# Row sums of squares for grouped-query heads: folded to 64 rows, two token tiles per product, issued in two groups

## The chip, the cores and the metric

The kernel runs on one core of a Trainium2 chip. The metric is device time in microseconds of one execution, the median of three. TensorE is called PE, VectorE DVE, ScalarE ACT, GpSimd POOL, SyncE SP, as in the profile.

## What is computed

One step of a two-layer backbone over 640 tokens (512 latent, 128 prompt), width 1024. Layer 0 mixes with latent attention and neighbourhood attention, layer 1 with grouped-query attention; each layer ends in a gated feed-forward block. The change lies in the attention of layer 1. Cut to that, the reference is:

```python
def odd_project(h, w_in, q_norm, k_norm):
    p = h @ w_in
    q, k, v = jnp.split(p, [...], axis=-1)
    q = rms_norm(q.reshape(b, L, GQA_HEADS, GQA_HEAD_DIM), q_norm)
...
def odd_mixer_latent(h, c_k, c_v, ...):
    q = apply_rope(q, cos, sin)
    k = apply_rope(k, cos, sin)
    o = attend_blocked(q, jnp.concatenate([k, c_k], axis=1),
                       jnp.concatenate([v, c_v], axis=1), GQA_SCALE)
```

There are 8 query heads of 128 features and 2 key heads. Each query row is divided by the root of its mean square. The kernel doesn't divide the queries: the factor of each token goes into the softmax, as the scale of the exponential.

## The kernel before

Features lie on the 128 partitions and the 640 tokens along the free axis, in two halves of 320 columns. A product in full precision is three products of split operands: each operand is kept as a high part and a low part in a rounded 32-bit type, and high*high, high*low and low*high add up in one PSUM bank. All products are recorded through one helper (line 64), all transposes through another (line 68), so PE's instructions are told apart by their tiles.

Layer 1's attention runs head by head. In the loop of head h the PE program holds pieces of three heads, in an order written out by hand as a string, `GQA_ORDER`:

```python
GQA_ORDER = "s0 r x0 t0 q0 s1 t1 q1 t2 s2 q2 v0 t3 s3 q3 v1 t4 s4 pt q4 v2 q5 q6 v3 q7 v4 pv"
```

- `s0` to `s4` are the scores of head h for five tiles of 128 tokens (tiles 0 to 3 latent, 4 prompt). Each writes a double bank `gs`; there are two of these, taken in turn, so `s2` waits until the exponential of tile 0 has read its bank. DVE takes the row maximum `gn` (lines 1873, 1879), a DVE product with the factor gives the bias `gb` (line 1883), and ACT writes the exponential `gp` (line 1884). `x0` is this second part of tile 0, kept apart in the string. In `s1` to `s4` it follows the scores directly.
- `q0` to `q7` project the queries of head h+1 (function `gqa_q`): four pieces for token columns 0 to 319, four for 320 to 639. After each half ACT copies the bank to `gqc` (line 1844) and squares the copy into `gsq` (line 1845). DVE applies the rotary tables in four instructions (`gqr`, lines 1748 to 1751, three of them before the closing addition), ACT rounds the result to `gqh` (line 1848), DVE takes the rest `gql` (line 1849).
- `r` sums the squares of head h over the 128 features: for each token tile a product whose stationary operand is the 128x128 block of `gsq` and whose moving operand is two columns of ones. These are plain 32-bit products, two passes each, so five products make ten passes, `gr`. ACT turns the sums into the factor `rq` by a logarithm and an exponential (lines 1856, 1857).
- `t0` to `t4` and `pt` transpose the probabilities of head h-1 (`gt`, `gtp`), ACT and DVE split them (`gts`, lines 401 and 405), and `v0` to `v4` and `pv` multiply them with the values (`go`, `gop`). POOL scales the probabilities beforehand (line 393).

Head 0 has no head before it, so its loop holds no `t` and no `v` piece. Its own queries are projected ahead of the loop. Head 7 has no head after it and holds no `q` piece. The compiler's scheduler orders each engine's own instructions from this program; each engine then works its queue in order.

## Time and profile before

| | us |
|---|---|
| runs | 1473.85, 1476.87, 1478.32 |
| median | 1476.87 |
| the profiled execution's own time | 1476.32 |
| its span, from the first to the last instruction | 1474.5 |
| PE busy | 1440.2 (98% of the span) |
| DVE busy | 1236.9 (84%) |
| ACT busy | 785.2 (53%) |
| grouped-query heads on PE, first scores to the first output projection | 849.5 to 987.4 |

Times in the rows further down are microseconds from the span's start. In a row of the timeline the first number is the start, the second how long the instructions of that row took together, and `[0.26 <-...]` behind it is how long the engine stood idle before it and what released it. PE's instructions overlap: a product of 320 columns is shown with 0.31 us, but the next one starts 0.15 us after it. What a product takes from the path is therefore read from one start to the next.

### The profile page before, as it was taken

To read this page: it belongs to the slowest core of one execution; us is meant where nothing else is said; L and a number is where in the kernel's file an instruction comes from. 1 tells how busy PE (TensorE), PEld (TensorE's weight loads), DVE (VectorE), ACT (ScalarE), POOL (GpSimd) and SP (SyncE) were. 2 spreads that over 40 slices of the span, in tenths; PEclk is the share of its full clock that TensorE was granted. 3 is DMA by queue.
4 is the path that set the end of the run, shared out by engine and by line. 5 is a ranking of instruction groups with operands and counts; after the bars stand their busy time and mean duration, and the time that the engine had idled before them with its cause. 6 is when DMAs were issued, how large, how long until landed. Compare 5 with 4: busy or idle time off the path is not lost.

```text
span 1474.5 us, 25830 instructions
## 1 busy us (share of the span) xinstructions
PE 1440.2 (98%) x9764; PEld 1389.8 (94%) x9764; DVE 1236.9 (84%) x2391; ACT 785.2 (53%) x1539; POOL 174.8 (12%) x270
## 2 busy tenths in 40 slices
PE   5999999999999999999999999999999999999997
PEld 3989978889999999999999999989999999999997
DVE  5877788877998888955997878888899898989976
ACT  5446687763755555531223656672656555555443
POOL 0046635420000000000000122220000000000000
PEclk9999999999999999999999999999999999999999
DMA  9644431025165555568764300115245555548572
GB/s 376 211 157 125 144 115 44 15 91 181 48 219 168 172 172 176 167 233 312 240 216 149 101 30 30 44 42 187 84 169 179 182 176 184 174 147 294 185 270 72
DMA packets 79636, 231.48 MB, mean 157 GB/s; under 512 B 8856, under 2 KB 13240, under 8 KB 79128
## 3 DMA queue, kind: packets, MB, share of 16 engines
q1 hardware_dynamic: 77152, 225.43, 45.5%
q10 hardware_dynamic: 1944, 3.48, 0.7%
q8 instruction: 76, 1.25, 0.3%
q0 software_dynamic: 416, 0.93, 0.2%
q14 instruction: 48, 0.39, 0.1%
HBM read 193.15 MB, written 36.66 MB: 156 GB/s over the span
## 4 chain that ended last, share of the span: by engine, by line
PE 86%; DVE 6%; ACT 4%; issue 2%; DMA 1%; POOL 1%; DVEq 0%; ACTq 0%; POOLq 0%; SPq 0%
PE fg L64 20%; PE fd L64 9%; PE fgo L64 5%; PE fo L64 5%; PE fu L64 4%; PE gq L64 4%; PE fdo L64 2%; PE gs L64 2%; PE go L64 2%; PE nq L64 2%; PE nk L64 1%; PE fuo L64 1%; PE gt L68 1%; PE mod L64 1%; ACT mp L1007 1%
## 5 line engine op out<-in xcount | busy, mean ns | idle before, releaser
L1679 DVE SCALAR_TENSOR_TENSOR junk<-wm,cb 128x1024 bf16<-128x1024 f32 x88 | 107.3, 1220 | 5.5 <-DMA wm<-in_wm 4.3
L64 PE MATMUL gq<-h10h,wgq 128*128 128x320 f32 x256 | 66.4, 319 | 0.0
L267 POOL TENSOR_SCALAR h10h<-h10t,gs,mods 128x320 fp32r<-128x320 f32 x4 | 4.0, 1006 | 430.2 <-DVE h10t L261 427.8
L1419 ACT ACTIVATE wY<-s 128x1024 fp32r<-128x1024 f32 x38 | 40.3, 1060 | 26.7 <-PE fg L64 22.5
L1947 POOL TENSOR_TENSOR xr<-xw,fn1rs 128x320 f32<-128x320 f32 x2 | 1.7, 868 | 412.8 <-ACT fn1rs L235 412.8
L1419 ACT ACTIVATE wZ<-s 128x1024 fp32r<-128x1024 f32 x38 | 40.2, 1057 | 19.1 <-PE fd L64 14.1
L1420 DVE TENSOR_TENSOR wZ<-s,wZ 128x1024 fp32r<-128x1024 f32 x38 | 46.4, 1221 | 2.0
L1420 DVE TENSOR_TENSOR wY<-s,wY 128x1024 fp32r<-128x1024 f32 x38 | 46.4, 1220 | 0.3
L64 PEld LDWEIGHTS gq<-h10h,wgq 128*128 128x128 f32 x256 | 45.4, 191 | 0.6
L1528 DVE TENSOR_TENSOR sg<-up,sg 128x640 f32<-128x640 f32 x38 | 31.3, 823 | 15.7 <-ACT sg L1527 14.7
L1527 ACT ACTIVATE sg<-fg 128x320 f32<-128x320 f32 x38 | 16.7, 439 | 48.3 <-PE fg L64 48.3
L1549 ACT ACTIVATE p<-fd 128x320 f32<-128x320 f32 x38 | 16.6, 438 | 46.0 <-PE fd L64 46.0
L64 PE MATMUL gq<-h10l,wgq 128*128 128x320 f32 x128 | 39.7, 311 | 0.0
L1884 ACT ACTIVATE gp<-gs,gb,rq 128x640 f32<-128x640 f32 (+1 forms) x40 | 31.8, 796 | 13.5 <-DVE gb L1883 12.0
L64 PE MATMUL fg<-h01E,wW 128*128 128x320 f32 x228 | 36.6, 309 | 1.5 <-DVE g L1559 1.5
L64 PE MATMUL fg<-h11N,wZ 128*128 128x320 f32 x228 | 36.7, 309 | 0.0
L64 PE MATMUL fg<-h01q,wX 128*128 128x320 f32 x228 | 36.7, 309 | 0.0
L64 PE MATMUL fu<-h11q,wX 128*128 128x320 f32 x228 | 36.6, 309 | 0.0
L64 PE MATMUL fg<-h01N,wZ 128*128 128x320 f32 x228 | 36.6, 309 | 0.0
L64 PE MATMUL fd<-h01q,wZ 128*128 128x320 f32 x228 | 36.6, 309 | 0.0
L64 PE MATMUL fd<-h11q,wZ 128*128 128x320 f32 x228 | 36.6, 309 | 0.0
L64 PE MATMUL fg<-h11q,wX 128*128 128x320 f32 x228 | 36.5, 309 | 0.0
(3421 smaller groups left out, 5303.3 us busy)
## 6 DMA issues: line engine op xcount, KB each, us to landing
wm<-in_wm SPq DMA_DIRECT2D x48, 512.0 KB, 4.1
mraw<-in_wm SPq DMA_DIRECT2D x8, 1024.0 KB, 13.2
mraw<-in_wm SPq DMA_DIRECT2D x14, 512.0 KB, 3.8
wmv<-in_wm0g SPq DMA_DIRECT2D x8, 512.0 KB, 4.2
wm<-in_wm0g SPq DMA_DIRECT2D x8, 512.0 KB, 4.9
ruo<-in_wFO SPq DMA_DIRECT2D x8, 512.0 KB, 4.3
rgo<-in_wFO SPq DMA_DIRECT2D x8, 512.0 KB, 5.6
x<-in_xT SPq DMA_DIRECT2D x8, 320.0 KB, 4.5
```

The source lines that it names most:

```text
L64: cls.last = nc.tensor.matmul(*a, **k)
L68: cls.last = nc.tensor.transpose(*a, **k)
L267: G.tensor_scalar(h[:, c0:c1], t, self.gsl[:, k, 0:1], self.ml[:, self.sh + k, 0:1], ALU.mult, ALU.add)
L1007: exps[h, j] = S.activation(halves(pt), pss[:, :, :HT], AF.Exp, bias=nm, accum_out=ll[:, j:j + 1])
L1419: S.activation(h, src, AF.Copy)
L1420: V.tensor_tensor(w_, src, f(h), ALU.subtract)
L1527: last = S.activation(sg[:, 0:HT], g[:, :HT], AF.Silu, scale=-1.0)
L1528: V.tensor_tensor(sg, up, sg, ALU.mult)
L1549: S.activation(p5, b5[:, :HT], AF.Copy)
L1679: V.scalar_tensor_tensor(junk, raw, 1.0, cb[:, c, :], ALU.mult, ALU.mult, accum_out=mods[l][:, j0 + i, c:c + 1])
L1884: gexp[h, j] = S.activation(dst, src, AF.Exp, bias=nb, scale=rq[:, j:j + 1], accum_out=ll[:, j:j + 1])
L1947: G.tensor_tensor(x[k][:, c0:c1], root[1][k], nrm.rs[:, c0:c1], ALU.mult)
```

## The change

The sum over 128 features is halved on DVE first. ACT squares the two halves of the feature rows (rows 0 to 63 and 64 to 127) into two tiles that both lie on partitions 0 to 63, by two instructions in place of one. DVE adds the two tiles and writes the result of one token tile to partitions 0 to 63 of a new tile `gfold`, that of the next to partitions 64 to 127. A product over 128 rows then sums two token tiles at once: its moving operand `two` has ones in rows 0 to 63 of its first column and in rows 64 to 127 of its second. Five products become three, of which the last (tile 4) has 64 rows. They are issued in two groups: tiles 0 and 1 by a piece `n` at the end of the loop of the head before, tiles 2 to 4 by `r`, which moves behind `q1`. The logarithm and the exponential for the factor run once for each group. The product of maximum and factor, `gb`, moves from DVE to ACT. In the second half `gql` comes behind the additions.

```diff
--- before.py
+++ after.py
@@ -1829,33 +1829,52 @@
     nc.gpsimd.dma_start(o_gv, gvf[:, :256])
 
     gqs, gexp = {}, {}
+    two = gp.tile([P, 2], F32, name="two")
+    V.memset(two, 0.0)
+    for r in range(2):
+        V.memset(two[64 * r:64 * r + 64, r:r + 1], 1.0)
 
     def gqa_q(h):
         get = lazy(lambda: after(gqs[h - 1][3][0] if h > 1 else None, lambda: unit(wGQ[h], 1024, f"wgq{h}", lo="v" if h == 1 else "v")))
         qh = gp.tile([P, T], F32R, tag="gqh", bufs=2, name=f"gqh{h}")
         ql = gp.tile([P, T], F32R, tag="gql", bufs=2, name=f"gql{h}")
         rq = tiny.tile([P, 5], F32, tag="rq", bufs=2, name=f"rq{h}")
-        sq = tmp(f"gsq{h}")
+        sq = [tmp(f"gsq{h}{r}")[0:64] for r in range(2)]
+        fold = gp.tile([P, 3, P], F32, tag="gfold", bufs=2, name=f"gfold{h}")
+        a, b = [t.rearrange("p (j n) -> p j n", n=P) for t in sq]
         gqs[h] = qh, ql, rq, []
+
+        def folded(i, r, j, n):
+            V.tensor_tensor(fold[64 * r:64 * r + 64, i:i + n, :], a[:, j:j + 2 * n - 1:2, :], b[:, j:j + 2 * n - 1:2, :], ALU.add)
         out = []
         for c, (c0, c1) in enumerate(HALF):
             def done(ps, c=c, c0=c0, c1=c1):
                 qc = tp.tile([P, HT], F32, tag="u", bufs=7, name=f"gqc{h}{c}")
                 gqs[h][3].append(S.activation(qc, ps[:, :HT], AF.Copy))
-                S.activation(sq[:, c0:c1], qc, AF.Square)
+                for r in range(2):
+                    S.activation(sq[r][:, c0:c1], qc[64 * r:64 * r + 64], AF.Square)
                 qr = tp.tile([P, HT], F32, tag="u", bufs=7, name=f"gqr{h}{c}")
                 rope(qr, qc, vcol(V_GQ), c, f"gqr{h}{c}")
                 S.activation(qh[:, c0:c1], qr, AF.Copy)
-                V.tensor_tensor(ql[:, c0:c1], qr, f(qh[:, c0:c1]), ALU.subtract)
+                if c == 0:
+                    V.tensor_tensor(ql[:, c0:c1], qr, f(qh[:, c0:c1]), ALU.subtract)
+                    folded(0, 0, 0, 1)
+                    folded(0, 1, 1, 1)
+                else:
+                    folded(1, 0, 2, 2)
+                    folded(1, 1, 3, 1)
+                    V.tensor_tensor(ql[:, c0:c1], qr, f(qh[:, c0:c1]), ALU.subtract)
             out += pieces_of(f"gq{h}{c}", qbank, get, hh, hl, list(range(KT)), c0, c1, done)
 
-        def rstd():
-            pr = bank(f"gr{h}")
-            for j in range(5):
-                PE.matmul(pr[:, 2 * j:2 * j + 2], sq[:, P * j:P * j + P], ones[:, 0:2], start=True, stop=True)
-            S.activation(rq, pr[:, 0:10].rearrange("p (a b) -> p a b", b=2)[:, :, 0], AF.Ln, bias=eps, scale=1.0 / P)
-            S.activation(rq, rq, AF.Exp, bias=lnsc, scale=-0.5)
-        return out + [rstd]
+        def rstd(at):
+            pr = bank(f"gr{h}{at}")
+            for i in ((0,), (1, 2))[at]:
+                rows = slice(0, P if i < 2 else 64)
+                PE.matmul(pr[:, 2 * (i - at):2 * (i - at) + 2], fold[rows, i, :], two[rows], start=True, stop=True)
+            t = rq[:, (0, 2)[at]:(2, 5)[at]]
+            S.activation(t, pr[:, 0:2 + at], AF.Ln, bias=eps, scale=1.0 / P)
+            S.activation(t, t, AF.Exp, bias=lnsc, scale=-0.5)
+        return out + [lambda: rstd(0), lambda: rstd(1)]
 
     def gqa_scores(h, pts):
         v = h // 4
@@ -1880,7 +1899,7 @@
                 dst, n = pt, P
 
             def weigh():
-                V.tensor_tensor(nb, nm, rq[:, j:j + 1], ALU.mult)
+                S.activation(nb, nm, AF.Copy, scale=rq[:, j:j + 1])
                 gexp[h, j] = S.activation(dst, src, AF.Exp, bias=nb, scale=rq[:, j:j + 1], accum_out=ll[:, j:j + 1])
                 softmax_tail(pt, ll[:, j:j + 1], f"gr{h}_{j}", n)
                 pts.append(pt)
@@ -1914,17 +1933,17 @@
         return {"pt": prompt_t, "pv": prompt, **t}
 
     open_y(s=2)
-    *qp, rstd = gqa_q(0)
-    run(qp)
+    *qp, early, rstd = gqa_q(0)
+    run(qp + [early])
     tail, oG = {}, []
-    GQA_ORDER = "s0 r x0 t0 q0 s1 t1 q1 t2 s2 q2 v0 t3 s3 q3 v1 t4 s4 pt q4 v2 q5 q6 v3 q7 v4 pv"
+    GQA_ORDER = "s0 x0 t0 q0 s1 t1 q1 r t2 s2 q2 v0 t3 s3 q3 v1 t4 s4 pt q4 v2 q5 q6 v3 q7 v4 pv n"
     for h in range(8):
         oG.append(gp.tile([P, T], F32, tag="go", bufs=8, name=f"oG{h}"))
         pts = []
         pieces = gqa_scores(h, pts)
         pieces["r"] = rstd
         if h < 7:
-            *qp, rstd = gqa_q(h + 1)
+            *qp, pieces["n"], rstd = gqa_q(h + 1)
             pieces.update(named("q", qp))
         sequence(GQA_ORDER, {**pieces, **tail})
         tail = gqa_values(h, pts, oG[h])
```

On PE, at the start of head 4's loop (`gs4_0` are its first scores, `gop2` the last values of head 2, `gt3` transposes of head 3, `gq5` queries of head 5), the order was before:

```order
L64 MATMUL gs4_0_10977<-gkh1_9590,gqh4_10730 128x320 x2
L64 MATMUL gs4_0_10977<-gkl1_9592,gqh4_10730 128x320 x2
L64 MATMUL gs4_0_10977<-gkh1_9590,gql4_10731 128x320 x2
L64 MATMUL gr4_10986<-ones_86,gsq4_10733 128x2 x5
L68 MATMUL gt3_0_10999<-ident_81,gp3_0_10737 128x128
```

With the change it is:

```order
L64 MATMUL gop2_11012<-gtp2l_10960,gvh5_9719 128x128
L64 MATMUL gr40_11017<-two_9993,gfold4_10778 128x2
L64 MATMUL gs4_0_11031<-gkh1_9590,gqh4_10773 128x320 x2
L64 MATMUL gs4_0_11031<-gkl1_9592,gqh4_10773 128x320 x2
L64 MATMUL gs4_0_11031<-gkh1_9590,gql4_10774 128x320 x2
L68 MATMUL gt3_0_11045<-ident_81,gp3_0_10782 128x128
```

The five products behind the first scores are gone; one stands ahead of them. The other two stand behind the second query piece, in head 0 directly ahead of the scores of tile 2.

On ACT, in head 0 (`gqc01` is the copy of the second half of its queries, `gp0_0` the exponential of its tile 0), the order was before:

```order
L1844 ACTIVATE gqc01_10067<-gq01_10042 128x320
L1845 ACTIVATE gsq0_10000<-gqc01_10067 128x320
L1856 ACTIVATE rq0_9999<-gr0_10095,eps_88 128x5
L1857 ACTIVATE rq0_9999<-rq0_9999,lnsc_90 128x5
L1848 ACTIVATE gqh0_9997<-gqr01_10070 128x320
L1884 ACTIVATE gp0_0_10087,gl0_10079<-gs0_0_10086,gb0_0_10085,rq0_9999 128x640
```

With the change it is:

```order
L1853 ACTIVATE gqc01_10076<-gq01_10051 128x320
L1875 ACTIVATE rq0_10003<-gr00_10090,eps_88 128x2
L1855 ACTIVATE gsq00_10004<-gqc01_10076 64x320
L1855 ACTIVATE gsq01_10005<-gqc01_10076 64x320
L1876 ACTIVATE rq0_10003<-rq0_10003,lnsc_90 128x2
L1858 ACTIVATE gqh0_10001<-gqr01_10080 128x320
L1875 ACTIVATE rq0_10003<-gr01_10152,eps_88 128x3
L1902 ACTIVATE gb0_0_10103<-gn0_0_10102,rq0_10003 128x1
L1876 ACTIVATE rq0_10003<-rq0_10003,lnsc_90 128x3
L1903 ACTIVATE gp0_0_10105,gl0_10095<-gs0_0_10104,gb0_0_10103,rq0_10003 128x640
```

The first exponential now stands behind the logarithm of the second group (`gr01`), which it doesn't need, and behind its own bias `gb0_0`, which was DVE's.

On DVE, in the same place (`gqr01` is the rotary result of the second half, `gn0_0` the row maximum of tile 0), the order was before:

```order
L1750 SCALAR_TENSOR_TENSOR gqr01b_10071<-gqc01_10067,vec_79,tg_9587 64x320
L1873 TENSOR_REDUCE gn0_0_10084<-gs0_0_10086 128x1
L1751 TENSOR_TENSOR gqr01_10070<-gqr01_10070,gqr01b_10071 128x320
L1883 TENSOR_TENSOR gb0_0_10085<-gn0_0_10084,rq0_9999 128x1
L1873 TENSOR_REDUCE gn0_1_10120<-gs0_1_10122 128x1
L1849 TENSOR_TENSOR gql0_9998<-gqr01_10070,gqh0_9997 128x320
```

With the change it is:

```order
L1750 SCALAR_TENSOR_TENSOR gqr01b_10081<-gqc01_10076,vec_79,tg_9587 64x320
L1848 TENSOR_TENSOR gfold0_10006<-gsq00_10004,gsq01_10005 64x256
L1751 TENSOR_TENSOR gqr01_10080<-gqr01_10080,gqr01b_10081 128x320
L1848 TENSOR_TENSOR gfold0_10006<-gsq00_10004,gsq01_10005 64x128
L1892 TENSOR_REDUCE gn0_0_10102<-gs0_0_10104 128x1
L1866 TENSOR_TENSOR gql0_10002<-gqr01_10080,gqh0_10001 128x320
```

The row maximum of tile 0 moved behind two of the new additions and the closing addition of the rotary step.

## Rows read from the trace of the kernel before

**Rows 1.** Page: busy time, share of the span and instructions of each engine.

```profile
PE 1440.2 (98%) x9764; PEld 1389.8 (94%) x9764; DVE 1236.9 (84%) x2391; ACT 785.2 (53%) x1539; POOL 174.8 (12%) x270
```

**Rows 2.** Page: the chain that ended last, shares by engine.

```profile
PE 86%; DVE 6%; ACT 4%; issue 2%; DMA 1%; POOL 1%; DVEq 0%; ACTq 0%; POOLq 0%; SPq 0%
```

**Rows 3.** Stretches: length, then PE, PEld, DVE, ACT, POOL busy, granted clock, DMA share, GB/s.

```profile
842.00:865.00 23.00, 22.37 (x155) 21.41 (x154) 19.00 (x45) 12.76 (x32) 5.07 (x7) 1.00 0.10 29
865.00:869.00 4.00, 4.00 (x20) 3.99 (x20) 2.62 (x6) 2.44 (x6) 0.00 (x0) 0.57 0.22 88
869.00:973.00 104.00, 104.00 (x713) 99.30 (x711) 85.93 (x189) 68.57 (x158) 24.64 (x30) 1.00 0.11 36
```

**Rows 4.** PE's timeline, heads 3 and 4: the ten passes, and what follows them.

```profile
901.70 1.17 PE L64 MATMUL gr<-ones,gsq 128*128 128x2 f32 x10
902.74 0.64 PE L68 MATMUL gt<-ident,gp 128*128 128x128 f32 x4
...
905.32 0.39 PE L64 MATMUL gq<-h10h,wgq 128*128 128x320 f32 x1
...
919.77 1.17 PE L64 MATMUL gr<-ones,gsq 128*128 128x2 f32 x10
```

**Rows 5.** PE's timeline, heads 0 and 1.

```profile
849.52 0.54 PE L64 MATMUL gs<-gkh,gqh 128*128 128x320 f32 x2
...
854.10 0.31 PE L64 MATMUL gq<-h10h,wgq 128*128 128x320 f32 x1
854.55 0.56 PE L64 MATMUL gs<-gkh,gqh 128*128 128x320 f32 x2
...
861.98 0.31 PE L64 MATMUL gq<-h10h,wgq 128*128 128x320 f32 x1
862.52 0.56 PE L64 MATMUL gs<-gkh,gqh 128*128 128x320 f32 x2 [0.23 <-ACT gqh L1848]
...
863.63 0.56 PE L64 MATMUL gs<-gkh,gql 128*128 128x320 f32 x2 [0.26 <-DVE gql L1849]
...
865.05 0.90 PE L68 MATMUL gt<-ident,gp 128*128 128x128 f32 x4
...
869.20 0.39 PE L64 MATMUL gq<-h10h,wgq 128*128 128x320 f32 x1
```

**Rows 6.** DVE's timeline, head 0: row maximum, closing addition of the rotary step.

```profile
851.90 0.82 DVE L1873 TENSOR_REDUCE gn<-gs 128x1 f32<-128x640 f32 x1
852.64 0.48 DVE L1751 TENSOR_TENSOR gqr<-gqr,gqr01b 128x320 f32<-128x320 f32 x1
```

**Rows 7.** ACT's timeline, head 0: the factor's exponential, the first of the softmax.

```profile
852.00 0.30 ACT L1857 ACTIVATE rq<-rq,lnsc 128x5 f32<-128x5 f32 x1
...
853.54 0.87 ACT L1884 ACTIVATE gp<-gs,gb,rq 128x640 f32<-128x640 f32 x1
```

**Rows 8.** Groups with shapes apart: count, busy us, mean ns, idle before.

```profile
L1883 DVE TENSOR_TENSOR gb<-gn,rq 128x1 f32<-128x1 f32 x40 | 6.6, 165 | 0.2
...
L754 DVE TENSOR_TENSOR nk<-nk,nk 64x256 fp32r<-64x256 f32 x8 | 3.4, 422 | 0.3
...
L879 DVE TENSOR_TENSOR kTl<-mk,kTh 64x128 fp32r<-64x128 f32 x6 | 1.7, 279 | 0.1
...
L1856 ACT ACTIVATE rq<-gr,eps 128x5 f32<-128x5 f32 x8 | 2.1, 267 | 9.7 <-PE gr L64 9.7
...
L724 ACT ACTIVATE nqh<-nq 64x64 fp32r<-64x64 f32 x8 | 1.7, 215 | 2.4 <-DVE nql L725 1.4 <-PE nq L64 1.0
```

**Rows 9.** The same, the squares, over the heads' stretch (842 to 985).

```profile
L1845 ACT ACTIVATE gsq<-gqc 128x320 f32<-128x320 f32 x16 | 7.5, 470 | 0.3
```

**Rows 10.** PE's timeline, head 7: its first wait.

```profile
979.96 0.56 PE L64 MATMUL gs<-gkh,gqh 128*128 128x320 f32 x2 [0.23 <-ACT gp L1884]
```

**Rows 11.** PE's timeline, layer 0: a long wait.

```profile
203.60 0.50 PE L64 MATMUL no<-nts_0l,nv 128*128 128x512 f32 x1 [1.75 <-DVE nts_0l L405]
```

**Rows 12.** Stretches as in rows 3: the microsecond behind that wait.

```profile
204.00:205.00 1.00, 0.72 (x7) 0.57 (x5) 0.91 (x5) 1.00 (x6) 0.50 (x1) 1.00 0.79 298
```

## The prediction

> **What bounds the kernel now.** I read the page first: PE is busy 98% of the span [rows 1], and the chain that ended last is 86% PE [rows 2]. So time is won where PE's own path gets shorter, and lost where PE begins to wait. Then I read the heads by stretches [rows 3]. From 869 to 973 PE shows no idle time at all, with DVE busy 85.93 of 104 us and ACT 68.57. Added work on these two has room there, as long as it doesn't come late for PE. The stretch before, 842 to 865, has idle time on PE (22.37 of 23), and the four microseconds from 865 run at a mean granted clock of 0.57, between the two levels: a spell at 1.2 GHz with full speed at its edges. The profiled execution took 1476.32 us, 0.55 under the median of the runs, 1476.87. The sum is made against 1476.32.
>
> **Fewer passes on PE.** The ten passes for the sums of squares hold PE from 901.70 to 902.74, where the next instruction starts [rows 4]: 1.04 us a head, 0.104 a pass. Three products are six passes, 0.62, so 0.42 a head is saved, and 3.3 over eight heads. No row shows such passes in two small groups. If each group leaves behind it what the ten do (they end 0.13 after their successor starts [rows 4]), the second group costs 0.13 more, and 2.3 is saved; if one pass of each group hides behind the long product ahead of it, 5.0. I take 3.3, the row itself, since a pass of two columns gives nothing to hide behind. The last product has only 64 rows, and no row shows a load of 64 rows; I price it like the others. The Trainium skill (TensorE: Matmul & The Clock Gate, section LDWEIGHTS) says that a weight load takes its time from the columns and not from the rows. By that rule the price of the third product stands; if half the rows were half the time, the sum would be 0.8 better.
>
> **More work on ACT and DVE.** ACT gets two more squares a head (0.47 each [rows 9]; halving the rows halves nothing in the free axis), a second logarithm and a second exponential (0.27 [rows 8], 0.30 [rows 7]) and five biases of 128x1. No row has such a bias on ACT. Above it lies 0.27 for 128x5 out of PSUM, below it DVE's own 0.165; I take 0.215, the 64x64 copy, which has the least work of ACT's copies in the rows [rows 8]. That is some 2.6 us a head. DVE gets three additions of 64x128 (0.28) and one of 64x256 (0.42) [rows 8], less the five biases of 0.165 [rows 8], so 0.4 more. In a row of DVE instructions the next one starts 0.08 before the last one's end (851.90 plus 0.82 against 852.64 [rows 6]), so I count 0.20 and 0.34. In the steady heads all this lies beside PE. Setting `two` is three small DVE instructions in the feed-forward layer before, where the chain is PE's: nothing, and 0.5 at 0.165 each if DVE were on the path there. No transfer moves in this stage.
>
> **Head 0, the new wait.** Here no transposes fill PE's queue, so I follow the chain to the scores of tile 2 (`gs2`), which need the bank that tile 0's exponential frees. Before, they started at 854.55, 0.30 after their place in the queue (854.10 plus the 0.15 from one start to the next) [rows 5]. Now PE comes to them earlier: from 849.52 to 854.25 are 4.73, less 1.04, plus 0.62 for the six passes that now all stand ahead, so at 853.84. But DVE goes from the three rotary instructions, over at 851.90 [rows 6], through 0.34, 0.40 for the closing addition and 0.20 before it starts the row maximum at 852.84, which ends at 853.66 (before: 852.72). ACT is by then stopped at the logarithm of the second group, which waits for the passes that end at 853.84, and works on in order: 0.27, bias 0.215, exponential 0.30, then `gp` of 0.87 [rows 7, 8], to 855.50. PE goes on 0.14 later, as it did before (853.54 plus 0.87 against 854.55 [rows 5, 7]), at 855.64. The wait is 1.8 in place of 0.3: 1.5 lost. Behind the waiting scores the rest of head 0, from the third query piece on, stands in PE's queue. If the logarithm holds nothing up and the bias costs 0.165, `gp` ends at 854.70 and the loss is 0.7. If the bias costs 0.27 and the logarithm starts only when the passes' last 0.13 is over, it is 1.7. Between these I take the 1.5 of the order as it stands.
>
> **Head 1's entry.** Before, PE lost 0.39 ahead of the first scores (861.98 plus 0.15 against 862.52) and, since the third pair comes 0.70 behind the first, 0.41 before that pair (863.63) [rows 5]. Both wait for operands that follow the query copy of head 1. The new additions push `gql` back by their 0.40, while PE itself is 1.1 late from head 0; without a slower clock about 0.35 to 0.45 of the 0.80 stays, with a slower clock in head 0 nothing does. I take 0.8 won.
>
> **The clock.** In the profiled execution PE ran at half clock behind these waits and ten narrow passes: from 865.05 to 869.20 it took 4.15 for what takes 2.58 in head 3 (902.74 to 905.32) [rows 4, 5], so 1.57 lost. In head 1 the cause goes: fewer passes in one place and shorter waits. In head 0 a like one comes: four narrow passes and a wait of 1.8 right behind them, 2.2 together, against the 0.8 and 1.04 of head 1 before. I forecast that the fall moves from head 1 to head 0: nothing won or lost. That narrow idle spells alone do it is not settled: a wait of 1.75 in layer 0 [rows 11] was followed by full clock [rows 12].
>
> **Head 7** has no query pieces, and PE waits for exponentials already (0.23 [rows 10]). The exponentials' chain there gets the same additions as PE loses passes; I take the 0.42 of the first term as kept, with 0.5 to either side.
>
> **Sum:** 3.3 won on passes, 1.5 lost in head 0, 0.8 won at head 1's entry, clock even: 2.6 won. 1476.32 less 2.6 is **1473.7 us**, 0.2% under the median.
>
> **Rivals.**
> The clock doesn't fall at all: 1.57 more is won, 0.4 of head 1's wait comes back, so 3.8 won and 1472.5. For it speaks rows 11 and 12; against it the likeness to rows 5.
> It falls in both heads: 1.57 less, 1475.3. The Trainium skill (TensorE: Matmul & The Clock Gate, section A second HAM failure mode: psum-queue depth-cycling) tells of short idle times between groups of products, as PSUM banks are waited for, that send the clock back and forth. By that rule the wait for the bank in head 0 would cost a spell at half clock; the trace agrees in head 1 [rows 3] and disagrees in rows 11 and 12.
> Slower than before: the first exponential is late in every head, as in head 0. Later heads have three groups of four transposes more on PE's path ahead of `gs2`. From 902.74 to 905.32 [rows 4] stand two such groups and twelve products of 0.15, so a group takes 0.39 and three take 1.2. The second group's logarithm no longer stands ahead of the first exponential there either (in head 4 ACT has it two exponentials later), which takes off another half microsecond, so the 1.8 should vanish. It decides from the point where what ACT has more to do ahead of that exponential there (two copies of the values, two splits) eats up this relief. At the upper end of the head 0 chain, a wait of 2.0, less only part of the relief, 1.0 a head would be left: seven heads lose 7.0, and the kernel takes 1480.7. Against it speaks that ACT is idle a third of the stretch and DVE 17% [rows 3]; for it, that both work in strict order and ACT's squares now stand ahead of the factor.
> The saving isn't there: six passes in two groups take as long as ten in one, 3.3 less won, 1477.0. For it speaks only that no row shows them apart.
>
> **How the numbers follow.** Forecast 0.43; no fall 0.25; fall in both 0.13; nothing saved 0.08; late in every head 0.08; something not listed 0.03. A measurement of this kernel can tell about 0.3%, 4.4 us, from no change, so faster means under 1472.4. About half of the no-fall case lies there, and a little of the forecast's own spread (passes saved 2.3 to 5.0): 0.18. Slower means over 1481.3, the far end of the late case: 0.05. Same takes 0.77. The range goes from the no-fall case with the better end for the passes (1.7 more), 1470.8, to the no-saving case with head 0's upper end (0.2) and head 7's (0.5), 1477.7.
>
> **What would show it.** Right: six `gr` passes a head, in a group of two and one of four, some 0.2 and 0.4 from start to start; no wait of PE between 885 and 970; one wait for `gp` in head 0 of 1 to 2 us ahead of `gs2`, with `gql` no longer waited for in head 1; each of heads 2 to 6 shorter by 0.42 than the 18.07 from 901.70 to 919.77 [rows 4]. The forecast is wrong if PE waits for `gp` or `gr` in heads 2 to 6, if the additions make the piece `n` wait at a head's end, or if the granted clock is at half in two places.

## The result, and the profile after

| | before | after |
|---|---|---|
| median of 18 runs each, us | 1476.17 | 1480.04 |
| lowest and highest | 1473.33, 1478.89 | 1477.64, 1482.97 |
| the profiled execution's own time | 1476.32 | 1478.45 |
| its span | 1474.5 | 1476.7 |

The changed kernel takes 1.0028 of the time of the one before (95% interval 1.0022 to 1.0035): 3.9 us slower. The forecast was 2.6 faster, and 1480.04 lies above its range, which ended at 1477.7.

The page's busy times and the three stretches of [rows 1] and [rows 3] now read:

```profile
PE 1437.0 (97%) x9732; PEld 1385.7 (94%) x9732; DVE 1241.3 (84%) x2386; ACT 807.3 (55%) x1611; POOL 176.0 (12%) x270
```

```profile
842.00:865.00 23.00, 20.92 (x143) 20.21 (x141) 18.83 (x43) 15.60 (x43) 4.56 (x6) 1.00 0.07 25
865.00:869.00 4.00, 3.59 (x26) 3.58 (x27) 3.88 (x10) 2.21 (x6) 0.60 (x1) 1.00 0.42 135
869.00:973.00 104.00, 102.80 (x686) 97.00 (x685) 88.34 (x183) 83.38 (x212) 25.14 (x30) 1.00 0.11 36
```

PE is busy 3.2 us less and yet the end comes later: it waits more. From 869 to 973, where it never stood idle in [rows 3], 1.2 us of idle time have appeared, while ACT went from 68.57 to 83.38 us. The granted clock is 1.00 in all three. PE's waits from 845 to 1060 (engine, tile, what released it: us in all, how often, the longest):

```profile
PE gs L64 <- ACT gp L1903: 2.5, 2, 1.6
PE gq L64 <- ACT oG L1932: 1.0, 1, 1.0
PE gs L64 <- DVE gql L1860: 0.6, 1, 0.6
PE oc3a L64 <- DVE ocw L174: 0.5, 1, 0.5
PE gt L68 <- ACT oG L1932: 0.4, 1, 0.4
PE gr L64 <- DVE gfold L1848: 0.3, 1, 0.3
PE oc6a L64 <- DVE ocw L174: 0.3, 1, 0.3
PE gt L68 <- DVE gts_0l L405: 0.2, 1, 0.2
```

Five of these the prediction names nowhere: the query piece and the transposes that wait for the copy `oG`, the transposes that wait for the split `gts_0l`, and two products of the output projection (`oc3a`, `oc6a`) that wait for the split of their weights (`ocw`).

To put a price on each place I cut PE's timeline at the first instruction of a kind and take the time from cut to cut. This leaves out all that happens ahead of the first query product `gq`, where nothing was changed and where that cut alone falls anywhere from 840.7 to 846.0 us in the fourteen profiles of this study. The kernel before was profiled twice (the second is the last experiment), and the right-hand columns are experiments below.

| us, PE, from ... to | before | before, 2nd | after | gb on DVE | split alone | fold in 2 to 5 |
|---|---|---|---|---|---|---|
| first `gq` to head 0's scores | 7.03 | 7.04 | 7.25 | 7.25 | 7.39 | 7.40 |
| head 0 | 13.00 | 12.98 | 13.99 | 13.97 | 12.64 | 12.64 |
| head 1 | 20.19 | 18.66 | 18.89 | 19.07 | 18.61 | 18.36 |
| heads 2 to 5 | 72.27 | 72.26 | 71.75 | 71.07 | 72.21 | 71.29 |
| head 6 | 18.06 | 18.07 | 19.29 | 19.10 | 18.03 | 18.03 |
| head 7 to the first `oc0b` | 22.52 | 22.52 | 22.70 | 23.08 | 21.52 | 21.53 |
| `oc0b` to `oc2b` | 14.52 | 14.52 | 14.52 | 14.52 | 14.52 | 14.52 |
| `oc2b` to `ocnp` | 30.82 | 30.82 | 32.47 | 30.83 | 30.82 | 30.82 |
| `ocnp` to the end | 433.60 | 433.09 | 433.09 | 433.04 | 433.33 | 433.05 |
| sum | 632.01 | 629.96 | 633.95 | 631.93 | 629.07 | 627.64 |

With the order of the change, a head's first group of passes stands ahead of its first scores, so it counts in the row above its own; the first row is 0.2 to 0.4 longer for that reason alone. After less the second profile of before is 3.99, what the medians say (3.87). It is made of head 0 (+1.0), head 6 (+1.2), the output projection (+1.65) and 0.2 each in the first row, head 1 and head 7, less 0.5 won in heads 2 to 5. Four places of the timeline show what happened. PE in head 4, from the last values of the head before to the transposes behind the second group:

```profile
918.43 0.33 PE L64 MATMUL gr<-two,gfold 128*128 128x2 f32 x2
918.62 0.54 PE L64 MATMUL gs<-gkh,gqh 128*128 128x320 f32 x2
...
919.59 0.60 PE L68 MATMUL gt<-ident,gp 128*128 128x128 f32 x4
920.15 0.41 PE L64 MATMUL gq<-h10h,wgq 128*128 128x320 f32 x1
...
922.02 0.60 PE L68 MATMUL gt<-ident,gp 128*128 128x128 f32 x4
922.37 0.40 PE L64 MATMUL gq<-h10h,wgq 128*128 128x320 f32 x1
...
923.34 0.59 PE L64 MATMUL gr<-two,gfold 128*128 128x2 f32 x4
923.86 0.66 PE L68 MATMUL gt<-ident,gp 128*128 128x128 f32 x4
```

The passes stand where the prediction had them, two and four, 0.19 and 0.52 from start to start, where some 0.2 and 0.4 were forecast. But the first transposes are followed after 0.56 by the query piece, the second ones after 0.35: 0.2 lost, too short to be listed as a wait. In head 6 it is long. PE, and ACT ahead of it:

```profile
955.60 0.60 PE L68 MATMUL gt<-ident,gp 128*128 128x128 f32 x4
957.22 0.41 PE L64 MATMUL gq<-h10h,wgq 128*128 128x320 f32 x1 [1.02 <-ACT oG L1932]
```

```profile
954.79 1.06 ACT L173 ACTIVATE ocw<-ocw1r 128x1024 fp32r<-128x1024 f32 x1
955.74 0.94 ACT L1855 ACTIVATE gsq<-gqc 64x320 f32<-64x320 f32 x2
956.59 0.57 ACT L1932 ACTIVATE oG<-go 128x512 f32<-128x512 f32 x1
```

The piece `q0` takes the bank in which the values of the head before were summed, and ACT's copy `oG` frees it. Ahead of that copy ACT now has two squares in place of one, and PE gets there sooner, since the passes between the scores and `t0` are gone. In head 0, DVE and ACT ahead of the first exponential:

```profile
852.16 0.42 DVE L1848 TENSOR_TENSOR gfold<-gsq,gsq 64x256 f32<-64x256 f32 x1
852.50 0.48 DVE L1751 TENSOR_TENSOR gqr<-gqr,gqr01b 128x320 f32<-128x320 f32 x1
853.01 0.28 DVE L1848 TENSOR_TENSOR gfold<-gsq,gsq 64x128 f32<-64x128 f32 x1
853.33 0.82 DVE L1892 TENSOR_REDUCE gn<-gs 128x1 f32<-128x640 f32 x1
```

```profile
854.23 0.26 ACT L1875 ACTIVATE rq<-gr,eps 128x3 f32<-128x3 f32 x1 [0.75 <-PE gr L64]
854.39 0.28 ACT L1902 ACTIVATE gb<-gn,rq 128x1 f32<-128x1 f32 x1
854.58 0.29 ACT L1876 ACTIVATE rq<-rq,lnsc 128x3 f32<-128x3 f32 x1
854.77 0.87 ACT L1903 ACTIVATE gp<-gs,gb,rq 128x640 f32<-128x640 f32 x1
```

The row maximum ends at 854.15, and `gp` starts 0.6 behind it. And in the output projection DVE starts to split the weights of `oc3` at 1015.46, behind the residual product of `oc2b`, and ends at 1016.68; without the wait PE would be at them some 0.5 earlier than the 1016.73 at which it starts:

```profile
1015.46 1.22 DVE L174 TENSOR_TENSOR ocw<-ocw3r,ocw 128x1024 fp32r<-128x1024 f32 x1
```

In the kernel before, the same split stood ahead of that residual product, which started at 1014.10, and PE didn't wait for it:

```profile
1012.57 1.21 DVE L174 TENSOR_TENSOR ocw<-ocw3r,ocw 128x1024 fp32r<-128x1024 f32 x1
```

### The profile page after: what moved, and what is told of

The parts are those of the page before. It is cut to its first block, busy times and chain, and to the rows that moved or that the text cites. A ratio compares the mean times of both kernels' runs of the same rounds, so it can differ in the third digit from the quotient of the medians.

```text
span 1476.7 us, 25863 instructions
## 1 busy us (share of the span) xinstructions
PE 1437.0 (97%) x9732; PEld 1385.7 (94%) x9732; DVE 1241.3 (84%) x2386; ACT 807.3 (55%) x1611; POOL 176.0 (12%) x270
## 3 DMA queue, kind: packets, MB, share of 16 engines
q8 instruction: 76, 1.25, 0.3%
## 5 line engine op out<-in xcount | busy, mean ns | idle before, releaser
L64 PE MATMUL fg<-h11E,wW 128*128 128x320 f32 x228 | 36.5, 309 | 0.0
```

Of the source, the lines that this page charges most:

```text
L64: cls.last = nc.tensor.matmul(*a, **k)
```

## The experiments

The first four undo or do one part each, in five rounds against the kernel before. Ratios stand with their 95% intervals.

**gb back on DVE** (`gb_dve`).

```diff
-                S.activation(nb, nm, AF.Copy, scale=rq[:, j:j + 1])
+                V.tensor_tensor(nb, nm, rq[:, j:j + 1], ALU.mult)
```

> The changed kernel with one part undone: the product of row maximum and factor (gb) is back on DVE. Theory: the moved gb is what changed the order of the output projection, where PE now waits for the weight splits of oc3 and oc6 and falls from 0.80 to 2.23 us behind the kernel before; with gb on DVE the PE order there is that of before again and these 1.4 us come back, and head 0's chain gets shorter by 0.30 less 0.17. Head 0's wait for gp (1.6) and head 6's wait for the copy oG (1.0) stay. About 1478.4 us, ratio to before 1.0015. Rival A (splitting the products into two groups costs it all): no change, 1480.0. Rival B (gb costs it all): 1476 or less.

Measured: 1478.31, ratio 1.0022 (1.0012 to 1.0032). In the table, `oc2b` to `ocnp` is 30.83 again with no wait for a weight split, and heads 2 to 5 take 71.07: 17.77 each, no 0.2 behind `t0`. Head 6 is nearly as long as before this edit, but for another wait: the transposes wait 0.72 for DVE's split `gts_0l`. So gb's move costs 2.0 us in the profile: 1.65 in the output projection, 0.7 in heads 2 to 5 and 0.2 in head 6, while with it head 7 is 0.4 shorter (22.70 against 23.08) and head 1 0.2. The times alone don't show these 2.0, since the two intervals overlap (1.0022 to 1.0035 and 1.0012 to 1.0032). The rest of the loss stays elsewhere.

**The fold alone, in one group at the old place** (`fold_only`): three products behind the first scores, one logarithm and one exponential, the order string of before, gb on DVE.

```diff
-        def rstd(at):
-            pr = bank(f"gr{h}{at}")
-            for i in ((0,), (1, 2))[at]:
+        def rstd():
+            pr = bank(f"gr{h}")
+            for i in range(3):
...
-    GQA_ORDER = "s0 x0 t0 q0 s1 t1 q1 r t2 s2 q2 v0 t3 s3 q3 v1 t4 s4 pt q4 v2 q5 q6 v3 q7 v4 pv n"
+    GQA_ORDER = "s0 r x0 t0 q0 s1 t1 q1 t2 s2 q2 v0 t3 s3 q3 v1 t4 s4 pt q4 v2 q5 q6 v3 q7 v4 pv"
```

> The fold alone: squares by halves, additions, three products, but all six passes in one group at the old place (behind the first scores), one logarithm and one exponential, gb on DVE. Theory: a group has a fixed price of about 0.1 us besides its passes, so one group of six takes about 0.65 in place of 1.03 and 0.35 a head is won, 2.8 in eight; the second square delays the copy oG by 0.5, but the passes still stand ahead of the query piece that needs that bank, so no wait for oG, or a few tenths in head 6 alone. Head 0 waits for the additions in place of the squares, 0.3 to 0.5 lost. About 1474 us. Rival A (six passes take as long as ten, or the extra ACT and DVE work costs as much): 1476 to 1478. Rival C (the fold itself makes the loss): 1479 or more.

Measured: 1500.78, ratio 1.0178 (1.0165 to 1.0191), the largest miss of my expectations. PE's first wait of the list and the stretch of heads 3 to 7:

```profile
PE gr L64 <- DVE gfold L1848: 15.0, 8, 3.3
```

```profile
900.00:987.00 87.00, 79.56 (x494) 75.99 (x493) 66.62 (x148) 53.76 (x121) 16.58 (x21) 0.92 0.12 37
```

In each head the products stand at PE until the additions are there, for 1.4 to 3.3 us, 1.9 on the mean, and the mean granted clock falls to 0.92: behind seven of these eight waits stands a stretch at the lower level. The fold turns one square into two squares and additions in DVE's queue, so the sums come later than PE needs them at the old place. The order of the change, with the first two tiles' group at a head's end and the others' behind `q1`, is what makes the fold bearable. Whether it takes the two groups for that, or only the later place, no run shows: one group of six behind `q1` was not run.

**The split alone** (`split_only`): whole squares and ten passes in groups of four and six, at the places of the change, gb on DVE.

```diff
-            for j in range(5):
-                PE.matmul(pr[:, 2 * j:2 * j + 2], sq[:, P * j:P * j + P], ones[:, 0:2], start=True, stop=True)
+            j0, j1 = (0, 2, 5)[at:at + 2]
+            for j in range(j0, j1):
+                PE.matmul(pr[:, 2 * (j - j0):2 * (j - j0) + 2], sq[:, P * j:P * j + P], ones[:, 0:2], start=True, stop=True)
...
+    GQA_ORDER = "s0 x0 t0 q0 s1 t1 q1 r t2 s2 q2 v0 t3 s3 q3 v1 t4 s4 pt q4 v2 q5 q6 v3 q7 v4 pv n"
```

> The split alone: full squares and ten passes as before, but in two groups at the places of the change (four passes at a head's end, six behind the second query piece), two logarithms and two exponentials, gb on DVE. Theory: the second group's own price is 0.15 to 0.2 a head, 1.2 to 1.6 in all, and in head 0 the first exponential stands behind the second logarithm, 1 to 1.5 more; PE comes to the first query piece 0.4 to 0.6 earlier, but the copy oG isn't later, so no wait for oG. About 1479 us. Rival C (the fold, by its second square and additions, makes the loss): 1476 to 1477.

Measured: 1474.55, ratio 0.9994 (0.9982 to 1.0005). No loss: the second group costs nothing that can be seen (heads 2 to 5 72.21 against 72.26), and head 7 is 1.0 shorter. Head 0 is 0.34 shorter, but the row above it is 0.35 longer by the group that moved there. The rival was right, the loss belongs to the fold and to gb.

**gb alone on ACT in the kernel before** (`gb_act`).

```diff
-                V.tensor_tensor(nb, nm, rq[:, j:j + 1], ALU.mult)
+                S.activation(nb, nm, AF.Copy, scale=rq[:, j:j + 1])
```

> The kernel before with one part of the change: gb on ACT. Theory: it is the change of the output projection's order, with waits for the splits of oc3 and oc6, and 0.13 more in the chain of a late exponential (0.30 on ACT in place of 0.17 on DVE) where PE waits for one, in heads 0 and 7. About 1.4 plus 0.4, 1478.0 us. Rival A (gb is beside PE everywhere): 1476.2. If the order of the output projection has nothing to do with gb, PE shows no wait for a split there.

Measured: 1475.92, ratio 1.0010 (1.0001 to 1.0018). The waits of the output projection are there with this edit alone:

```profile
PE oc3a L64 <- DVE ocw L174: 0.5, 1, 0.5
...
PE oc6a L64 <- DVE ocw L174: 0.2, 1, 0.2
```

`oc2b` to `ocnp` takes 32.26, against 30.82. The products between are the same 210 in both; around the wait of 0.51 PE loses some 0.8 from start to start, around that of 0.2 some 0.5, and two products of `oc4b`, which now stand ahead of the first wait, another 0.2. The whole is less than the 1478.0 I expected: the profile has head 0 0.4 shorter (12.54) and head 1 0.4 longer (19.10), and head 7 0.4 shorter (22.12). The compiler's scheduler has written DVE's and PE's order in the output projection anew, some 30 us behind the last `gb`. One bias took 0.163 on DVE and takes 0.29 on ACT. The Trainium skill (Perfetto Trace Analysis, section Optimizing Scalar/DVE Operations) says that work may go to ACT where DVE is saturated; by that rule this move could have paid. The traces agree in head 7, which is 0.4 shorter with it in both pairs of kernels; over the whole program no run shows a gain.

The others look into single places.

**Head 7 not folded** (`fold_allbut7`), gb on DVE.

```diff
+        folds = h < 7
...
-                for r in range(2):
+                for r in range(2 if folds else 0):
                     S.activation(sq[r][:, c0:c1], qc[64 * r:64 * r + 64], AF.Square)
+                if not folds:
+                    S.activation(sq[:, c0:c1], qc, AF.Square)
```

> Split in two groups and fold for heads 0 to 6, gb on DVE; head 7's squares stay whole, with five products in the two groups. Theory: with the fold in all heads the loss sits at the two ends of the heads: head 0, and heads 6 and 7, where ACT and DVE also split the weights and the operands of the output projection (head 6 19.10 and from head 7's first scores to oc0b 23.08 us, against 18.03 and 21.52 with the split alone). Without the fold of head 7 these come back, 1.0 and 1.0 to 1.5: some 2 to 2.5 us under the kernel that has only gb undone, ratio to before about 1.0005. Rival (a loss of the fold that every head shares): 0.3 to 0.5 us back, ratio 1.002.

Measured: 1476.05, ratio 1.0013 (1.0003 to 1.0022). Head 7 to `oc0b` goes from 23.08 to 21.51: the expected 1.5. Head 6 doesn't come back (19.34). So it pays for its own fold and not for that of head 7; the run with the fold in heads 2 to 5 alone, further down, has 18.03 there. The second half of its fold lies at its entry, where DVE also splits two weights of the output projection, and the additions stand between these and the row maximum. With gb undone alone that is:

```profile
959.36 1.23 DVE L174 TENSOR_TENSOR ocw<-ocw1r,ocw 128x1024 fp32r<-128x1024 f32 x1
960.50 0.49 DVE L1751 TENSOR_TENSOR gqr<-gqr,gqr61b 128x320 f32<-128x320 f32 x1
960.91 0.71 DVE L1848 TENSOR_TENSOR gfold<-gsq,gsq 64x256 f32<-64x256 f32 x2
961.64 0.82 DVE L1892 TENSOR_REDUCE gn<-gs 128x1 f32<-128x640 f32 x1
```

**The first query piece behind the second scores** (`q0_later`), in the changed kernel.

```diff
-        sequence(GQA_ORDER, {**pieces, **tail})
+        sequence(GQA_ORDER.replace("q0 s1", "s1 q0") if h else GQA_ORDER, {**pieces, **tail})
```

> The changed kernel with one exchange in the order of heads 1 to 7: the first query piece comes behind the scores of tile 1. Theory: in the changed kernel this piece waits for the bank that the copy oG frees, 0.2 in each of heads 3 to 5 and 1.0 in head 6, since the second square goes ahead of that copy on ACT and the passes no longer stand ahead of the piece. Behind the second scores it comes 0.9 later, so heads 3 to 5 take 17.77 in place of 18.0 and head 6 loses at most 0.3 of the 1.2: 1.5 won, 1478.5. Rival (the copy is not what it waits for, or the next wait takes its place at the scores of tile 2): heads 3 to 6 stay as long, 1480.

Measured: 1479.04, ratio 1.0036 (1.0023 to 1.0049). Heads 3 and 4 take 17.76 and 17.79 in place of 17.98 and 18.00, so the wait for the bank was that 0.2. Head 5 stays at 17.97, and head 6 grows to 19.70: its transposes now wait 0.7 for `gts_0l`, and `oG` is still waited for, 0.5. The wait was named rightly, but in head 6 the next one takes its place.

**The second logarithm behind the first exponential, in head 0 alone** (`ln_later`), in the changed kernel; one profile.

```diff
-            S.activation(t, pr[:, 0:2 + at], AF.Ln, bias=eps, scale=1.0 / P)
+            after(gexp[h, 0] if at else None, lambda: S.activation(t, pr[:, 0:2 + at], AF.Ln, bias=eps, scale=1.0 / P))
```

> The changed kernel with ACT's order changed in head 0 alone: the second logarithm and its exponential behind the first softmax exponential. My forecast had this order as the cause of 1.5 lost in head 0 (logarithm, bias, exponential ahead of gp). Now: in the trace gb starts 0.16 behind that logarithm's start, so the order costs 0.16 to 0.4 of the 1.59, and the rest is the row maximum, which stands behind three additions' worth of DVE and starts 853.33. Head 0 takes 13.6 to 13.8 in place of 13.99. Rival (the forecast's reading): 12.9 or less.

Measured: head 0 takes 13.80 in place of 13.99, the wait 1.4 in place of 1.6. The order on ACT was a seventh of the loss, not its cause.

**ACT's part of the fold alone** (`split_sq2`): the split alone with the squares in two instructions.

```diff
-                S.activation(sq[:, c0:c1], qc, AF.Square)
+                for r in range(2):
+                    S.activation(sq[64 * r:64 * r + 64, c0:c1], qc[64 * r:64 * r + 64], AF.Square)
```

> The split alone, and ACT squares by halves of the rows, two instructions in place of one, without folding: ACT's part of the fold without DVE's and PE's. Theory: ACT's extra 0.47 per half costs little while the copy oG still comes before it is needed: 0 to 0.3 in the steady heads, up to 0.5 in head 6, 0.3 in head 0; about 1475.5, 1 us over the split alone. The larger part of the fold's loss is DVE's additions. Rival (ACT's squares make the loss): 1477.5 or more, with waits of PE for oG and gp in heads 6 and 7 as in the changed kernel.

Measured: 1472.96, ratio 0.9993 (0.9984 to 1.0002). Of all stretches only head 6 changes, from 18.03 to 18.45.

**DVE's part alone** (`split_adds`): the split alone with the four additions added, their result unused.

```diff
+        fold = gp.tile([P, 3, P], F32, tag="gfold", bufs=2, name=f"gfold{h}")
+        a = sq[0:64].rearrange("p (j n) -> p j n", n=P)
...
+                else:
+                    folded(1, 0, 2, 2)
+                    folded(1, 1, 3, 1)
+                    V.tensor_tensor(ql[:, c0:c1], qr, f(qh[:, c0:c1]), ALU.subtract)
```

> The split alone with DVE's part of the fold added and nothing else of it: squares whole, all ten passes, and the four additions of the change at their places, their result unused. Theory: the additions of the second half, which DVE works off ahead of the first row maximum of a head, make most of the fold's loss: head 0 13.5 to 14 us in place of 12.64, head 6 18.5 to 19 in place of 18.03, head 7 14 to 15 in place of 13.50; from the queries' first product to the end 631 to 632 in place of 629.1, ratio to before 1.001 to 1.002. Rival (the lengthened chain, squares before additions before sums, makes it, not DVE's time): no more than 0.5 us over the split alone.

Measured: 1480.69, ratio 1.0035 (1.0021 to 1.0049). From the first `gq` to the end it takes 636.4, more than I gave, because in this profile the clock fell in heads 0 and 7 too. The wait for `gp` ahead of `gs2` is 1.55 in head 0, as with the whole fold, and ends at 855.16; in head 7 it is 1.84. Both falls come right behind these waits. In head 0:

```profile
852.00:855.00 3.00, 1.61 (x14) 1.53 (x12) 2.60 (x7) 1.79 (x5) 0.00 (x0) 1.00 0.00 0
856.00:859.00 3.00, 3.00 (x13) 3.00 (x12) 1.15 (x3) 0.97 (x2) 1.07 (x2) 0.50 0.00 0
```

Heads 0 and 7 take 15.58 and 24.71. Less the 1.5 that such a fall cost in head 1 of the kernel before, that is 14.1 and 23.2, an estimate, near the 13.97 and 23.08 of the whole fold. Head 6 is not longer (18.05). So the additions alone bring the waits in heads 0 and 7, and their loss but for the clock. In head 6 the squares alone cost 0.4, the additions alone nothing and both 1.1; how they add up there wasn't taken apart further.

**The additions behind the first row maximum** (`fold_f`): a piece `f` of the order behind `s0 x0`, gb on DVE.

```diff
-                    folded(1, 0, 2, 2)
-                    folded(1, 1, 3, 1)
...
+        def late():
+            folded(1, 0, 2, 2)
+            folded(1, 1, 3, 1)
...
+    GQA_ORDER = "s0 x0 f t0 q0 s1 t1 q1 r t2 s2 q2 v0 t3 s3 q3 v1 t4 s4 pt q4 v2 q5 q6 v3 q7 v4 pv n"
```

> The changed kernel with gb back on DVE and the additions of the second half put behind the row maximum of tile 0, by a piece of its own behind s0 and x0; all heads folded. Theory: the row maximum of a head's first tile then comes 0.7 earlier and the wait ahead of the scores of tile 2 in head 0 goes back to 0.3: head 0 12.7 to 13.0 us, head 6 at most 18.3, head 7 13.5, heads 2 to 5 17.77 as with gb alone undone. From the queries' first product to the end 627 to 628.5, against 629.1 with the split alone and 631.9 with gb alone undone; ratio to before 0.998 to 0.9995. Rival (the place of the additions doesn't matter, their amount or the squares do): 631 or more, ratio 1.001 to 1.002.

Measured: 1477.05, ratio 1.0006 (0.9997 to 1.0015). Head 0 takes 13.05 in place of 13.97, so there it was the additions' place. But heads 6 and 7 keep their loss (19.06 and 22.93), and there the products now wait, 0.52 and 1.34. The sum is 630.8, against 627 to 628.5 expected, near the rival's 631. PE's waits for the additions:

```profile
PE gr L64 <- DVE gfold L1848: 2.6, 4, 1.3
```

**The fold in heads 2 to 5 alone** (`fold_2to5`), with the split, gb on DVE: the edit of `fold_allbut7` with this line.

```diff
+        folds = 1 < h < 6
```

> Split in two groups, gb on DVE, and the fold only where PE never waits, for heads 2 to 5; heads 0, 1, 6 and 7 keep whole squares and their ten passes. Theory: the loss sits at the entries of heads 0, 1, 6 and 7; heads 2 to 5 keep the 0.28 that six passes save against ten, 1.1 in all: from the queries' first product to the end 628.0, ratio to before 0.9985. Rival (the fold's loss appears in whatever head has it first or last): an entry of head 2 or 5 takes 0.4 to 1 longer and the ratio is 0.9995 or more.

Measured: 1472.70, ratio 0.9982 (0.9973 to 0.9991): faster than both kernels. The sum of the table is 627.64, 2.3 under the second profile of before, 0.4 better than expected. The split alone has 0.9 of these 2.3; heads 2 to 5 give 0.9 more by their fewer passes, and the rest is in head 1, which holds the first passes of head 2, and in the stretch behind `ocnp`, which the edit doesn't touch. Against the split alone the times don't settle it, their intervals overlap (0.9982 to 1.0005). All waits of PE from 845 to 1060 are these:

```profile
PE gs L64 <- ACT gp L1915: 0.6, 2, 0.3
PE gop L64 <- DVE gtp6l L405: 0.4, 1, 0.4
PE gs L64 <- DVE gql L1866: 0.3, 1, 0.3
```

**The kernel before, profiled again** (`before_again`), without an edit.

> The kernel before, unchanged, profiled a second time. In its first profile the clock was granted at half between 865 and 869 us, which cost 1.57 us in head 1 (20.19 in place of 18.62). Of the changed kernel and ten variants, profiled once each, two show such a fall in the heads and another three or four show one in the first 250 us, where nothing was changed. Theory: the fall belongs to one execution and not to the waits in head 1; a second profile has head 1 at 18.6 us and from the queries' first product to the end 630.4. Rival (the waits and the ten passes bring it about each time, as my forecast had it): 20.2 and 632.0 again.

Measured: head 1 takes 18.66, and the sum is 629.96. The stretch that had a mean clock of 0.57 in [rows 3]:

```profile
865.00:869.00 4.00, 4.00 (x31) 3.98 (x30) 3.26 (x8) 3.15 (x7) 0.80 (x1) 1.00 0.00 0
```

The program is 1.75 earlier in this execution, but the clock is 1.00 in all the heads. The same instructions in the same order, with the same waits (0.3 for `gql`, 0.2 for `gqh`), at full clock. So the fall belonged to that one execution.

Of the eleven variants' profiles ten show such a fall in the first 250 us, more than I said, ahead of everything that was changed. Eight of these stand in one place, right behind the wait in layer 0 that [rows 11] show, there followed by full clock. With gb undone alone this wait is 1.74 and ends at 204.51, and a little later the stretch is:

```profile
207.00:210.00 3.00, 3.00 (x15) 3.00 (x15) 2.50 (x10) 1.94 (x8) 0.55 (x1) 0.50 0.00 0
```

All fourteen profiles have this wait, of 1.46 to 1.75 us, and six of them have full clock behind it, the two of the kernel before and that of the changed kernel among them. So the same wait is followed by a fall in one execution and not in another.

## Why the prediction was wrong

**Passes: the mechanism right, the size off.** The step took 0.42 a head "since a pass of two columns gives nothing to hide behind". With gb on DVE heads 2 to 5 take 17.77 in place of 18.07: 0.30 a head, 2.4 if all eight had it, near the lower bound of the term (2.3). Its reason was another, though. The second group costs nothing: with the split alone the groups of four and six take 0.41 and 0.58 from start to start in these heads, together no more than the 1.04 of the ten. A group's first pass does hide, since the second starts 0.03 behind it where a long product stands ahead. The fold brings the first group from 0.41 to 0.19, but the second, of four passes now, only from 0.58 to 0.52. What is dear is the last product, of 64 rows, "I price it like the others": its first pass starts 0.18 behind the pass ahead, its second 0.13 behind the first, and the transposes 0.18 behind that, where passes over 128 rows start 0.11 apart. That is 0.16 a head, 1.25 in eight, an estimate from these steps. The six passes of the split alone, and with gb undone alone the first pass of 64 rows and the transposes behind:

```profile
905.73 0.72 PE L64 MATMUL gr<-ones,gsq 128*128 128x2 f32 x6
```

```profile
908.72 0.27 PE L64 MATMUL gr<-two,gfold 64*128 64x2 f32 x1
909.03 0.33 PE L68 MATMUL gt<-ident,gp 128*128 128x128 f32 x1
```

**"In the steady heads all this lies beside PE": the step that failed.** I costed the added work on ACT and DVE by its sum against the idle share of a stretch of 104 us. It lies beside PE in heads 2 to 5, with gb on DVE. At the entry of head 6, where DVE has two weight splits to do and ACT their high parts, it doesn't: 1.0 to 1.2 lost. That these splits are the reason is argued from their place; the squares alone cost 0.4 there and the additions alone nothing. And with gb on ACT the copy `oG` comes 0.2 late in heads 3 to 5. I had not followed which bank the query piece takes once the passes no longer stand ahead of it. Head 7, which I gave 0.5 to either side, loses about 1.5 by the fold, which the split's own gain of 1.0 covers in part.

**gb on ACT: priced as five small instructions, not as a new schedule.** I took 0.215 for one; it takes 0.29. Beside that, with the edit the scheduler ordered the output projection otherwise, and there 1.65 was lost, in a place that my sum didn't enter. The order of the two kernels shows this without a run; the sum looked at the heads' order alone.

**Head 0: the place right, the cause half right.** I forecast a wait of 1.8 and 1.5 lost; the wait is 1.59, and head 0 is 1.0 longer with the passes' gain in it, so 1.3 by that chain. But I put the logarithm's place on ACT ahead of the additions. Of the loss the logarithm's place is 0.2 (`ln_later`) and the additions' place 0.9 (`fold_f`).

**Head 1: wrong.** I took 0.8 won, on the ground that PE would be late and the waits vanish. PE waits 0.31 for `gfold` and 0.59 for `gql`, 0.9 in all, and the head is 0.2 longer. PE's first scores of head 1 start 1.5 later than before (863.99 against 862.52), but the pair that needs `gql` starts 1.8 later (865.41 against 863.63). (0.26 of both lies ahead of the first query product.)

**The clock: even, for the wrong reason.** I took the fall at 865 for an effect of the waits and passes and let it move to head 0. It wasn't there when the same kernel was profiled again. After a wait of 1.59 in head 0 the clock of the changed kernel stays at 1.00. Luck has a part in that: with the additions alone a wait of 1.55 in the same place is followed by 0.50, and the wait in layer 0 by a fall in eight of fourteen profiles. What decides it in one execution stays open. The Trainium skill (TensorE: Matmul & The Clock Gate, section A second HAM failure mode: psum-queue depth-cycling) has short idle times between groups of products, as PSUM banks are waited for, send the clock back and forth. By that rule the wait for the bank in head 0 would cost a spell at 1.2 GHz. The trace of the changed kernel disagrees (1.00), that of the additions alone agrees (0.50). The fold alone at the old place has such spells too (0.92), though its eight waits are for additions and not for a bank.

**The rivals.** The case on the slower side named "the first exponential late in every head". It is late in heads 0 and 7 alone. The time came out near its 1480.7, by other means: two entries, one bank and one new schedule.

**The sum in these terms.** Against the second profile of before, with 0.30 a head for the passes, 2.4 were won. Lost were 1.3 in head 0, 0.5 in head 1, 0.7 behind `oG` in heads 3 to 5, 1.5 in head 6, 0.7 in head 7 and 1.65 in the output projection: 6.35, so 4.0 lost on balance. Of these losses the forecast held head 0's alone.

## What to carry to other kernels

Work beside the bottleneck is not priced by an engine's idle share over a long stretch. Look at the entries, where that engine already works without a gap, and ask which instruction of the chain to the bottleneck stands behind the added ones; a change that gains in the middle of a loop and loses at its edges can be kept for the middle, as fold 2 to 5 shows. Where a scheduler writes the order, moving one small instruction to another engine can reorder a stage far behind it, so the order there belongs to the reading too. And before a term is built on a dip of the clock in one profile, or on its absence behind a wait, take more profiles.

## What the runs showed of the hardware that I had not expected

- A bias of 128x1 takes 0.292 on ACT and 0.163 to 0.166 on DVE, and a square of 64x320 takes as long as one of 128x320 (0.468 and 0.469): half the partitions save nothing.

```profile
L1855 ACT ACTIVATE gsq<-gqc 64x320 f32<-64x320 f32 x32 | 15.0, 468 | 0.5
L1902 ACT ACTIVATE gb<-gn,rq 128x1 f32<-128x1 f32 x40 | 11.7, 292 | 11.0 <-DVE gn L1898 5.5 <-DVE gn L1892 4.8 <-DVE gr_1r L392 0.6
```

- A short wait of PE costs more than its idle row shows: a row of 0.51 cost some 0.8 from start to start, one of 0.2 to 0.3 some 0.5. Of that 0.16 is the overlap of two products (0.31 shown, 0.15 from start to start), which idle time doesn't count.
- Passes of two columns over 128 rows start 0.11 apart in a group; the steps into, inside and out of a product of 64 rows are 0.18, 0.13 and 0.18.
- Two profiles of the same kernel differ by 1.5 us in one head through the granted clock alone, and one wait of 1.46 to 1.75 us in layer 0 is followed by a fall of the clock in eight of fourteen profiles.
